# One line of the FFN: the difference of two resident weight granules on GpSimd instead of VectorE

## Chip, cores and metric

The kernel runs on one core of a Trainium2 chip. The metric is the device time of one execution in microseconds; the time of a kernel is the median of its runs. Engines are named as in the profile: PE (TensorE, matmuls) with PEld (its weight loads), DVE (VectorE), ACT (ScalarE), POOL (GpSimd) and SP (SyncE, which issues nearly all DMAs here).

## The reference

One layer of a diffusion backbone in float32: 384 tokens (128 context, 256 latent) of width 2048. adaLN modulation, a mixing sub-layer (gated linear attention beside a Fourier branch) and a SwiGLU FFN with 5632 hidden units. What matters here is the end:

```python
h = rmsnorm(x, lw['norm_pre_ffn']) * (1.0 + sc2) + sh2
ff = (jax.nn.silu(h @ lw['w_ffn_gate']) * (h @ lw['w_ffn_up'])) @ lw['w_ffn_down']
x = x + ga2 * rmsnorm(ff, lw['norm_post_ffn'])
```

## The kernel before

**Split products.** A float32 operand is used as two fp32r parts: ACT casts it to `hi` (`whi`, L1467 in the FFN), DVE makes `lo = src - hi` (`wlo`, L1478), and PE adds up hi·hi, hi·lo and lo·hi. Weights come in granules of 128x1024; each granule that PE uses costs one cast on ACT and one subtraction on DVE. `whi` and `wlo` have four buffers each, so up to four split granules lie ready ahead of PE.

**The FFN** (from about 920 us on) goes through the hidden units in 11 chunks of 512. Chunk 0 is plain. Chunks 1 to 10 compute gate and up with a scheme of fewer products: of the weights it uses granules and their sums and differences, so that seven products stand for eight in the two latent token tiles, while the context tile uses the same granules plainly. With `u` and `g` for up and gate, and 0 and 1 for the halves of the model dimension, the steps of chunk c are, with i = 0..3 for each kind:

- A: `u0` (slot x). B: the difference `g0 - u0`, which is put in x in place of `u0`.
- C: `g1` arrives in `raw`; x becomes `g1 - x` and y becomes `g1 - y` (L1474, L1475). E uses x, F uses y.
- G: `u1` arrives; x becomes `u1 - x` (L1477). H uses x.
- D: the down projection of the chunk before, interleaved with C to H.

PE needs 12 matmuls of 512 columns for an A, B, C or G, 6 for E, F or H, 18 for a D.

**Slots.** The granules of A and B are *resident*: eight slots of 128x1024 in SBUF (tiles named `u`), loaded by SP (L1445) as soon as `free` has them. x and y of a chunk are `slots[slot(0, c, i)]` and `slots[slot(1, c, i)]`; F frees y, H frees x. The other granules come through two `raw` buffers (L1437).

**What sets the order.** All five engines run an order written out by hand. `grab2` (per step) takes a ready granule for PE, runs what is due (`now`), lets SP load (`load_more`) and calls `split_next`, which issues the cast, up to three pending operations (`settle_pend`: evictions of finished PSUM banks, L1588 to L1629), then for this kind of step the differences, then the `wlo`. `split_next` runs about four granules ahead of PE. `sum1(c, i)`, the difference of A's and B's granules, is called early: `sum1(c, 0)` at granule A3, `sum1(c, i + 1)` at granule Bi, each ahead of that granule's `wlo`:

```python
ACT.copy(hi, src)
settle_pend()
if (kind, i) == ("A", 3):
    sum1(c, 0)
elif kind == "B" and i < 3:
    sum1(c, i + 1)
```

A side task, `ada_last` (L1507, L1509, L1531 to L1534), makes the last adaLN vector on DVE from `w_ada`, two DVE instructions a portion, and is stepped at A, G and late D steps, until chunk 9.

POOL does little: a few `memset`s, 15 additions (L1250) and two `wlo` (L228) between 890 and 915 us, and sixteen additions of 128x128 (L1762) in the last 20 us. In the tail, L1724 to L1726 are tiny DVE instructions on 128x1, and L1764 writes the output.

Tiles in SBUF: `u`, `raw`, `whi`, `wlo`, `ep` (gate and up sums), `acc`, `w`, `spad`, `psums` (running down sums), `bias`, `ssq`, `A_hi`, `A_lo`, `x1b`. Tiles in PSUM: `pgu`, `pdn`, `ptr`, `py`, `prow`, `z`, `zx`.

Of the kernel before, what the change touches and what calls it, by code (L numbers as in the profile page):

```python
# [96 lines left out]
def tile_step(ctx: ExitStack, tc: tile.TileContext, a, o):  # L97
    nc = tc.nc
    PE, ACT, DVE, POOL, SP = nc.tensor, nc.scalar, nc.vector, nc.gpsimd, nc.sync
# [776 lines left out]
    with ExitStack() as s:  # L876
# [207 lines left out]
        for b, i in mix_order:  # L1084
# [9 lines left out]
            else:  # L1094
# [4 lines left out]
                g, y = gates.pop((b, i))  # L1099
# [14 lines left out]
    with ExitStack() as s:  # L1114
# [309 lines left out]
        def slot(x, c, i):  # L1424

            return 4 * ((c + x) % 2) + i
# [21 lines left out]

        def sum1(c, i):
            x, y = (slots[slot(n, c, i)] for n in range(2))  # L1450
            DVE.tensor_sub(x, y, x)  # L1451

        def settle_pend():
            for _ in range(3):
# [3 lines left out]
        def split_next():  # L1458

            if not entries:  # L1460
                settle_pend()
                return
            kind, c, i, raw = entries.pop(0)
            x, y = (slots[slot(n, c, i)] if kind not in "RD" else None for n in range(2))
            src = raw if kind in "RCGD" else y if kind == "F" else x
            hi, lo = (wp.tile([P, G], F32R, tag=t, name=t, bufs=4) for t in ("whi", "wlo"))
# [6 lines that stand above are left out]
            elif kind == "C":  # L1473
                DVE.tensor_sub(x, raw, x)  # L1474
                DVE.tensor_sub(y, raw, y)  # L1475
            elif kind == "G":
                DVE.tensor_sub(x, raw, x)  # L1477
            DVE.tensor_sub(lo, src, hi.bitcast(F32))  # L1478
            if kind in "RCGD":
                out_now[0] -= 1  # L1480
            elif kind == "F":
                free.add(slot(1, c, i))
            elif kind == "H":
                free.add(slot(0, c, i))
            ready.append((hi, lo))
# [417 lines left out]
```

## Time and profile before

| what | value |
|---|---|
| time before, median of 3 runs | 1954.05 us (1953.54 to 1954.51) |
| profiled execution, span from first to last instruction | 1950.6 us |
| around the span (median less span) | 3.4 us |
| PE busy | 1936.3 us (99%), 10422 matmuls |
| DVE busy | 1633.1 us (84%), 2114 instructions |
| ACT busy | 906.9 us (46%), 1270 instructions |
| POOL busy | 33.6 us (2%), 55 instructions |
| granted TensorE clock, mean | 0.999 |

"Busy" is the time in which an engine runs at least one instruction; matmuls are pipelined, so 99% says that they follow each other without gaps, not that PE is at its peak. The page gives groups of instructions as `line engine op out<-in shape xcount | busy us, mean ns | idle time ahead of them`. A timeline row is `start us, duration us, engine, line, operation, out<-in, shape, xcount`, with an `x2` or more for instructions in a row that are merged. A row of one line's instructions gives `xcount: min/median/max ns, first to last start`. The profile gives one execution; the time of the program lies above its span by what surrounds it.

### The profile page before, as it was taken

Reading aid. Unit: us, or ns where it says so; the run is one execution under the profiler, and the core shown is the slowest. Engines: PE = TensorE matmul, PEld = TensorE weight load, DVE = VectorE, ACT = ScalarE, POOL = GpSimd, SP = SyncE. Lnnn points to the kernel's source line nnn. Section 1 sums busy time; section 2 is a strip of 40 time slices with the busy share of each in tenths; the row PEclk is TensorE's granted clock in tenths of the full one; section 3 lists DMA queues with packets and bytes.
Section 4 is the critical chain, followed back from the end, with each engine's and each line's share of the span. In section 5 each row is a group of like instructions: output and inputs, shape, how many; then the busy total and the mean of one; then the engine's idle time right before and its main releaser. Section 6 shows DMA issues by size and latency. Waiting matters only on the chain.

```text
span 1950.6 us, 27243 instructions
## 1 busy us (share of the span) xinstructions
PE 1936.3 (99%) x10422; PEld 1705.2 (87%) x10422; DVE 1633.1 (84%) x2114; ACT 906.9 (46%) x1270; POOL 33.6 (2%) x55
## 2 busy tenths in 40 slices
PE   9999999999999999999999999999999999999998
PEld 5779999999889999999988888888888888888886
DVE  5668888878777797977789898999898999887876
ACT  4233554544336654446454444444444444444444
POOL 0000000000000000004000000000000000000001
PEclk9999999999999999999999999999999999999999
DMA  9978677767765786655355535463636263626244
GB/s 391 382 255 272 228 257 239 231 218 244 239 198 178 236 265 212 233 188 210 93 157 162 172 125 179 137 199 112 199 120 209 93 216 98 211 75 194 67 157 144
DMA packets 201179, 380.12 MB, mean 195 GB/s; under 512 B 14160, under 2 KB 127508, under 8 KB 196696
## 3 DMA queue, kind: packets, MB, share of 16 engines
q1 hardware_dynamic: 200520, 378.12, 58.4%
q8 instruction: 82, 1.34, 0.3%
q14 instruction: 49, 0.40, 0.1%
q10 hardware_dynamic: 528, 0.26, 0.0%
HBM read 361.55 MB, written 16.78 MB: 194 GB/s over the span
## 4 chain that ended last, share of the span: by engine, by line
PE 96%; DVE 2%; DMA 2%; ACT 1%; issue 0%; SPq 0%; POOL 0%; DVEq 0%; ACTq 0%; POOLq 0%
PE pmm L261 32%; PE pgu L273 30%; PE pdn L273 18%; PE pfo L273 3%; PE pv L415 3%; PE pgm L398 1%; PE pf L1064 1%; PE pmm L1320 1%; DMA slab<-in_w_ada 1%; PE ptr L1612 1%; PE pf L1065 1%; PE po L673 1%; DMA xraw<-in_w_x 0%; PE px L433 0%; DMA raw<-in_w_d 0%; DVE x1b L1764 0%
## 5 line engine op out<-in xcount | busy, mean ns | idle before, releaser
L261 PE MATMUL pmm<-A_hi,whi 128*128 128x384 f32 x1072 | 361.3, 337 | 0.0
L261 PE MATMUL pmm<-A_hi,wlo 128*128 128x384 f32 x1072 | 358.6, 335 | 0.0
L261 PE MATMUL pmm<-A_lo,whi 128*128 128x384 f32 x1072 | 358.5, 334 | 0.0
L1467 ACT CAST whi<-u 128x1024 fp32r<-128x1024 f32 x200 | 210.6, 1053 | 271.0 <-DVE u L1451 86.2
L227 ACT CAST whi<-raw 128x1024 fp32r<-128x1024 f32 x181 | 189.5, 1050 | 208.1 <-DMA raw<-in_w_gate 69.0
L1467 ACT CAST whi<-raw 128x1024 fp32r<-128x1024 f32 x175 | 184.2, 1053 | 212.1 <-DMA raw<-in_w_g 68.0
L228 DVE TENSOR_TENSOR wlo<-raw,whi 128x1024 fp32r<-128x1024 f32 x179 | 218.1, 1221 | 66.2 <-ACT whi L227 65.5
L1478 DVE TENSOR_TENSOR wlo<-u,whi 128x1024 fp32r<-128x1024 f32 x200 | 243.9, 1220 | 28.1 <-ACT whi L1467 16.9
L273 PE MATMUL pgu<-whi,A_hi 128*128 128x512 f32 x640 | 250.0, 391 | 0.0
L273 PE MATMUL pgu<-whi,A_lo 128*128 128x512 f32 x640 | 249.3, 389 | 0.0
L1478 DVE TENSOR_TENSOR wlo<-raw,whi 128x1024 fp32r<-128x1024 f32 x175 | 213.3, 1219 | 33.9 <-ACT whi L1467 24.6
L600 DVE SCALAR_TENSOR_TENSOR adacc<-adaw,spad,adacc 128x1024 f32<-128x1024 f32 x180 | 222.8, 1279 | 0.3
L261 PEld LDWEIGHTS pmm<-A_hi,whi 128*128 128x128 f32 x1072 | 201.2, 188 | 3.0 <-issue 1.4
L261 PEld LDWEIGHTS pmm<-A_lo,whi 128*128 128x128 f32 x1072 | 201.3, 188 | 0.3
L261 PEld LDWEIGHTS pmm<-A_hi,wlo 128*128 128x128 f32 x1072 | 201.2, 188 | 0.0
L273 PE MATMUL pdn<-whi,hid_hi 128*128 128x512 f32 x480 | 186.9, 389 | 0.0
L273 PE MATMUL pdn<-whi,hid_lo 128*128 128x512 f32 x480 | 186.8, 389 | 0.0
L273 PE MATMUL pgu<-wlo,A_hi 128*128 128x512 f32 x640 | 184.2, 389 | 0.0
L273 PEld LDWEIGHTS pgu<-whi,A_hi 128*128 128x128 f32 x640 | 120.1, 188 | 26.0 <-issue 0.8
L273 PEld LDWEIGHTS pgu<-wlo,A_hi 128*128 128x128 f32 x640 | 120.1, 188 | 25.4
L273 PEld LDWEIGHTS pgu<-whi,A_lo 128*128 128x128 f32 x640 | 120.1, 188 | 25.0
L273 PE MATMUL pgu<-whi,S 128*128 128x512 f32 x480 | 131.1, 395 | 0.0
(386 smaller groups left out, 2900.0 us busy)
## 6 DMA issues: line engine op xcount, KB each, us to landing
adaw<-in_w_ada SPq DMA_DIRECT2D x96, 512.0 KB, 4.1
raw<-in_w_d SPq DMA_DIRECT2D x88, 512.0 KB, 4.6
slab<-in_w_ada SPq DMA_DIRECT2D x32, 1024.0 KB, 10.4
raw<-in_w_gate SPq DMA_DIRECT2D x64, 512.0 KB, 4.7
raw<-in_w_g SPq DMA_DIRECT2D x48, 512.0 KB, 4.2
raw<-in_w_u SPq DMA_DIRECT2D x48, 512.0 KB, 3.8
raw<-in_w_in SPq DMA_DIRECT2D x44, 512.0 KB, 4.2
u<-in_w_u SPq DMA_DIRECT2D x40, 512.0 KB, 4.4
```

The source lines that it names most:

```text
L227: ACT.copy(hi, raw)
L228: sub = lambda: eng.tensor_sub(lo, raw, hi.bitcast(F32))
L261: PE.matmul(dst, w[wi][:, k * n + n0 : k * n + n0 + P], x[xi][:, k0 + k, :], start=first and k == 0 and j == 0, stop=last and k == kts - 1 ...
L273: PE.matmul(dst, stat[x_][m], mov(w[w_], m), start=first and w_ == m == x_ == 0, stop=last and w_ == m == 1,)
L398: PE.matmul(pgv[q : q + 32, :], spad[:, k, :], slab[k // (KT // 2)][:, k % (KT // 2), :], start=k < 4, stop=k >= KT - 4,)
L415: PE.matmul(pv[2 * t + g], hT[x_][:, kb, t * P : (t + 1) * P], w_[:, g * 512 : (g + 1) * 512], start=kb == 0 and j == 0, stop=kb == KT - 1 ...
L600: DVE.scalar_tensor_tensor(acc[:, c, :], w, spad[:, k, c : c + 1], acc[:, c, :], op0=ALU.mult, op1=ALU.add,)
L673: PE.matmul(dst, w[wi], x[xi], start=first and j == 0, stop=last and j == 2)
L1064: PE.matmul(pf[:, 0 : 2 * HT], w[0][:, c], x[k], start=k == 0, stop=False)
L1065: PE.matmul(pf[:, 0:HT], w[1][:, c], x[k][:, 0:HT], start=False, stop=m == 1 and k == 3)
L1467: ACT.copy(hi, src)
L1478: DVE.tensor_sub(lo, src, hi.bitcast(F32))
```

## The change

`sum1` issues its subtraction on POOL. Nothing else is edited. In the order of instructions, the 40 subtractions (4 in each of chunks 1 to 10) leave DVE's queue and stand in POOL's queue in the same order, between its last L228 and its first L1762. Each waits there for the loads of its two granules and for DVE's `wlo` of its A granule. The ACT cast (L1467) of a B granule waits for POOL where it waited for DVE. PE's, ACT's and SP's orders are the same as before.

```diff
         def sum1(c, i):
             x, y = (slots[slot(n, c, i)] for n in range(2))
-            DVE.tensor_sub(x, y, x)
+            POOL.tensor_sub(x, y, x)
```

## Prediction

> **What bounds the kernel now.** I read the head of the page, then the chain of work that ended last, then the busy time by stretches.
>
> ```profile
> span 1950.6 us, 27243 instructions
> ```
> ```profile
> PE 96%; DVE 2%; DMA 2%; ACT 1%; issue 0%; SPq 0%; POOL 0%; DVEq 0%; ACTq 0%; POOLq 0%
> ```
> ```profile
> 960.00:1900.00 940.00, 940.00 (x4255) 776.39 (x4254) 841.54 (x913) 429.47 (x465) 0.00 (x0) 1.00 0.47 149
> 1231.00:1264.00 33.00, 33.00 (x153) 27.30 (x152) 32.42 (x39) 12.26 (x15) 0.00 (x0) 1.00 0.29 94
> ```
>
> The rows of the last fence give, after the length of the stretch, busy time of PE, PEld, DVE, ACT and POOL, then granted clock and DMA. From 960 to 1900 us, where all ten FFN chunks of this change run, PE is busy 940.00 of 940.00 us at a clock of 1.00: matmuls stand back to back, and nothing that another engine gives up can make this stretch shorter. DVE has 841.54 us of work in it (90%) and POOL none. But the mean hides a tight place: in the 33 us around the four differences of chunk 4, DVE is busy 32.42 us. There DVE is the local limit, and PE lives on the four split weight tiles made ahead. So the question is not what DVE saves, but whether the new place of the difference can make a tile arrive later than its **slack**: the time from the end of its wlo instruction (L1478) to the first matmul that reads this wlo.
>
> **The change, part by part.**
>
> ```profile
> L1451 DVE TENSOR_TENSOR u<-u,u x40: 1212/1217/1219, 963.6 to 1816.5; 128x1024 f32<-128x1024 f32 x40
> ```
> ```profile
> L228 POOL TENSOR_TENSOR wlo<-raw,whi 128x1024 fp32r<-128x1024 f32 x2 | 4.8, 2397 | 0.0
> ```
>
> *Removed:* 40 differences on DVE, four in each of ten chunks, 1.217 us each; the next instruction starts 1.13 us after such a one (1245.73 to 1246.86 below), so DVE's queue gets 1.13 us shorter at each, 45 us in all. PE was never short of work in this stretch, so this alone is worth 0.
>
> *Added:* 40 instructions on POOL. The nearest row is the same shape and subtraction on POOL, 2.397 us; I take 2.40. 40 of them make 96 us in 940, on an engine with no work there.
>
> *Moved, and the new waits:* POOL's queue holds nothing but these differences between its last L228 and the sixteen L1762 of the tail, and it issues no DMA. A difference starts as soon as granule A of its pair has been split (both its casts and its wlo) and the loads of both granules are in; on DVE it stood three granules later. So it is ready long before the cast of granule B, which now waits for POOL instead of DVE: in chunk 4 below, A0's wlo ends at 1235.25; 2.40 us later would be 1237.65, where DVE finished this difference at 1246.95. Late results are therefore no cost. The loads into the slots keep their order on SP's queue and stay released by later splits (L1467, L1478). ACT's queue behind that cast is unharmed for the same reason.
>
> *The cost that I do expect:* POOL's work holds up DVE. The row for it is in the tail.
>
> ```profile
> L1725 DVE TENSOR_TENSOR bias<-bias,ssq x3: 160/160/358, 1925.9 to 1938.3; 128x1 f32<-128x1 f32 x3
> ```
> ```profile
> 1938.34 0.36 DVE L1725 TENSOR_TENSOR bias<-bias,ssq 128x1 f32<-128x1 f32 x1
> ```
> ```profile
> 1938.22 0.46 POOL L1762 TENSOR_TENSOR x1b<-x1b,ep 128x128 f32<-128x128 f32 x1 [2.29 <-ACT ep L1761]
> ```
>
> One tiny DVE instruction runs three times: 160, 160 and 358 ns. The long one started 0.12 us into a POOL instruction and ended at 1938.70, 0.02 us after POOL's (1938.68). It reads two tensors from SBUF; so does that POOL instruction. It was held 0.20 us, to about 1938.53, which is 0.15 us before POOL's end. Against it stand DVE instructions that read one tensor from SBUF and the other from PSUM (z, prow, pgu and pdn are PSUM tiles):
>
> ```profile
> L1302 DVE TENSOR_TENSOR A_lo<-z,A_hi x13: 550/557/558, 893.7 to 915.5; 128x384 fp32r<-128x384 f32 x13
> ```
> ```profile
> 907.05 2.40 POOL L228 TENSOR_TENSOR wlo<-raw,whi 128x1024 fp32r<-128x1024 f32 x1
> ```
> ```profile
> 908.04 0.56 DVE L1302 TENSOR_TENSOR A_lo<-z,A_hi 128x384 fp32r<-128x384 f32 x1
> ```
>
> The one at 908.04 lies wholly inside a 2.40 us POOL subtraction and takes its usual time. So I take it that a POOL subtraction holds DVE only where DVE's next instruction reads two SBUF tensors, for up to 2.40 - 0.15 = 2.25 us. This rests on a single held instruction; the bounds of a hold are therefore 0 and 2.40 us.
>
> The Trainium skill, "SBUF — State Buffer", section "Who interferes with whom", states the same as a rule against this change: a VectorE instruction with two SBUF inputs contends with a GpSimd instruction that reads SBUF, through a shared port that is held for a whole instruction, and the second one fully blocks. The long L1725 agrees with it; by the rule to the letter the hold would be 2.40 us, without it 0.
>
> Now the place. DVE's queue in chunk 4, from A0's wlo to B0's (L1478 is the wlo of A0, A1, A2, A3, B0 in turn), and the first matmul that reads B0's wlo:
>
> ```profile
> 1234.03 1.22 DVE L1478 TENSOR_TENSOR wlo<-u,whi 128x1024 fp32r<-128x1024 f32 x1
> 1235.17 1.41 DVE L1509 SCALAR_TENSOR_TENSOR acc<-w,spad,acc 128x512 f32<-128x512 f32 x2
> 1236.49 0.68 DVE L1601 TENSOR_TENSOR ep<-ep,pgu 128x512 f32<-128x512 f32 x1
> 1237.21 0.69 DVE L1601 TENSOR_TENSOR ep<-ep,ep 128x512 f32<-128x512 f32 x1
> ...
> 1238.41 1.22 DVE L1478 TENSOR_TENSOR wlo<-u,whi 128x1024 fp32r<-128x1024 f32 x1
> 1239.55 0.68 DVE L1602 TENSOR_TENSOR ep<-ep,ep 128x512 f32<-128x512 f32 x1
> 1240.15 0.68 DVE L1605 TENSOR_TENSOR ep<-ep,pgu 128x512 f32<-128x512 f32 x1
> 1240.86 0.69 DVE L1605 TENSOR_TENSOR ep<-ep,ep 128x512 f32<-128x512 f32 x1
> 1241.47 1.22 DVE L1478 TENSOR_TENSOR wlo<-u,whi 128x1024 fp32r<-128x1024 f32 x1
> 1242.61 1.41 DVE L1509 SCALAR_TENSOR_TENSOR acc<-w,spad,acc 128x512 f32<-128x512 f32 x2
> 1243.93 1.88 DVE L1629 TENSOR_TENSOR psums<-psums,pdn 128x512 f32<-128x512 f32 x3
> 1245.73 1.22 DVE L1451 TENSOR_TENSOR u<-u,u 128x1024 f32<-128x1024 f32 x1
> 1246.86 1.22 DVE L1478 TENSOR_TENSOR wlo<-u,whi 128x1024 fp32r<-128x1024 f32 x1
> 1248.00 1.41 DVE L1509 SCALAR_TENSOR_TENSOR acc<-w,spad,acc 128x512 f32<-128x512 f32 x2
> 1249.32 1.22 DVE L1451 TENSOR_TENSOR u<-u,u 128x1024 f32<-128x1024 f32 x1
> 1250.46 1.22 DVE L1478 TENSOR_TENSOR wlo<-u,whi 128x1024 fp32r<-128x1024 f32 x1
> ```
> ```profile
> 1253.35 0.61 PE L273 MATMUL pgu<-wlo,S 128*128 128x512 f32 x2
> ```
>
> Each difference starts after the L1478 of its A granule, when DVE's next instruction has already begun; I let POOL have its turn after that one. Difference 0 then falls on the second L1509: held 2.25. Difference 1 starts after L1602; the first L1605 (one operand in PSUM) passes, the second is held 2.25 - 0.65 = 1.6. Differences 2 and 3 each fall on a second L1509: 2.25 each. Sum before B0: 2.25 + 1.6 + 2.25 + 2.25 = 8.35 us. By then two differences have left the queue, 2.27 us. B0's wlo is later by 8.35 - 2.27 = 6.1 us. Its slack is 1253.35 - (1250.46 + 1.22) = 1.67 us, so PE waits 6.1 - 1.7 = **4.4 us** in chunk 4. The tiles after B0 come off better: each drops another 1.13 us, and PE's wait has moved them too.
>
> The other chunks, by DVE's end and PE's first use:
>
> ```profile
> 1059.79 1.22 DVE L1478 TENSOR_TENSOR wlo<-u,whi 128x1024 fp32r<-128x1024 f32 x1
> ...
> 1628.22 1.22 DVE L1478 TENSOR_TENSOR wlo<-u,whi 128x1024 fp32r<-128x1024 f32 x1
> ...
> 1436.14 1.22 DVE L1478 TENSOR_TENSOR wlo<-u,whi 128x1024 fp32r<-128x1024 f32 x1
> ```
> ```profile
> 1064.47 0.61 PE L273 MATMUL pgu<-wlo,S 128*128 128x512 f32 x2
> ...
> 1631.11 0.62 PE L273 MATMUL pgu<-wlo,S 128*128 128x512 f32 x2
> ...
> 1439.51 1.07 PE L273 MATMUL pgu<-wlo,A_hi 128*128 128x512 f32 x4
> ```
>
> Chunk 2, B0: slack 3.46, wait 6.1 - 3.5 = 2.6. Chunk 8, B0: slack 1.67, wait 4.4. Chunk 6 has no L1509 between A3 and B0, so its worst tile is A3: held 2.25 + 1.6 + 2.25 less 1.13 = 5.0, slack 2.15, wait 2.8. In chunks 3, 5, 7, 9 and 10 no L1509 stands behind A0 and A2, as in chunk 7:
>
> ```profile
> 1518.83 0.68 DVE L1601 TENSOR_TENSOR ep<-ep,pgu 128x512 f32<-128x512 f32 x1
> ...
> 1524.94 1.88 DVE L1629 TENSOR_TENSOR psums<-psums,pdn 128x512 f32<-128x512 f32 x3
> ...
> 1531.41 1.22 DVE L1478 TENSOR_TENSOR wlo<-u,whi 128x1024 fp32r<-128x1024 f32 x1
> ```
> ```profile
> 1537.17 0.62 PE L273 MATMUL pgu<-wlo,S 128*128 128x512 f32 x2
> ```
>
> Behind A0 and A2 PSUM readers pass (0.65 and about 1.8 us): holds 1.6 + 1.6 + 0.45 + 2.25 = 5.9, less 2.27, makes 3.6 us against a slack of 4.5: no wait. Chunk 1 runs its first three differences while DVE still idles: no wait. **Sum:** 4.4 + 2.6 + 4.4 + 2.8 = 14.2 us. On the profiled execution 1950.6 + 14.2 = 1964.8 us of span; the median of the runs, 1954.05, lies 3.4 us above that span, for what is around it, so the forecast is 1954.05 + 14.2 = **1968.2 us**.
>
> **The rivals.**
>
> *No hold.* The one long L1725 is chance, or a long POOL instruction lets DVE in. Then DVE is only relieved, PE is full as before, and the time is 1954.0. For it: one row carries the lock. Against it: that row ends with POOL's to 0.02 us, and no other cause is near. This is the case that ends on the other side: not slower, decided by whether L1478 keeps its 1.22 us, and a pair of L1509 its 1.41 us, beside POOL's differences.
>
> *A hold, but DVE keeps its turn.*
>
> ```profile
> L1467 ACT CAST whi<-u 128x1024 fp32r<-128x1024 f32 x200 | 210.6, 1053 | 271.0 <-DVE u L1451 86.2
> ```
>
> Consecutive DVE instructions start some 0.08 us before the one ahead ends (1235.17 before 1235.25), so POOL may get in only at a PSUM reader or a pause. Then L1509 is never held; holds before B0 are 1.6 + 1.6 + 0.45 (1.6 + 1.6 in chunk 2), less 2.27, under every slack. But difference 3 waits until DVE stands at B3 for want of the cast: 2.40 plus the 1.05 us cast, some 3.6, less the 0.9 that DVE is ahead by then, 2.7 late; against slacks of an estimated 0.4, 1.3 and 1.7 us at the next tile, C0 (chunks 4, 6, 8; the same subtraction of DVE's end from PE's first use), PE waits about 5 us: 1959.
>
> *Every difference holds its whole 2.40 us*, whatever stands next: 9.6 - 2.27 = 7.3 late at B0 in nine chunks, less B0's slacks of 1.7 (chunk 4) to an estimated 6.6 us (chunk 3), which the same subtraction gives: about 33 us in all, 1987.
>
> *Faster:* PE is busy 940.00 of 940.00 us of this stretch, so a gain over 0.2% (3.9 us) has nowhere to come from. That the change is not carried out is excluded: the order of instructions has 40 L1451 on POOL and none on DVE.
>
> **How the numbers follow.** The forecast of turns 0.48; DVE keeps its turn 0.17 (1959 is 0.26% up, so 0.10 of it counts as slower and 0.07 as the same); no hold 0.20; whole holds 0.12; faster 0.03. A measurement of this kernel tells about 0.2% from no change. Slower 0.48 + 0.10 + 0.12 = 0.70, same 0.27, faster 0.03. The range takes in no hold at its low end and half of the way from the forecast to whole holds at its high end: 1953.5 to 1981.
>
> **What would show it.** Right: L1451 on POOL near 2.4 us; beside it L1478, L1509 and the second L1601 and L1605 up to 2.2 us longer, L1629 not; waits of PE (or PEld) for wlo L1478 in chunks 2, 4, 6 and 8, none before. Wrong: DVE's durations unchanged beside POOL (no hold), or POOL's instructions stretched and late with DVE's kept (DVE's turn), or PE waiting for ACT's cast behind POOL.

## The result, and the profile after

The changed kernel took 1974.3 us (median of 4 runs, 1973.7 to 1978.0) beside 1953.8 us before (1952.7 to 1954.5): a ratio of 1.0109, 95% interval 1.0097 to 1.0121. It is 20.5 us slower. The forecast was 1968.2 us, 14.2 us slower. The profiled execution has a span 21.1 us longer than before (1971.7 against 1950.6). The page of the changed kernel: span, busy time of the engines, the chain of work that ended last, and the group of the differences.

```profile
span 1971.7 us, 27281 instructions
...
PE 1939.1 (98%) x10422; PEld 1704.6 (86%) x10422; DVE 1654.4 (84%) x2074; ACT 908.4 (46%) x1270; POOL 141.5 (7%) x95
...
PE 89%; DVE 7%; DMA 2%; issue 2%; ACT 1%; SPq 0%; POOL 0%; DVEq 0%; ACTq 0%; POOLq 0%
...
L1451 POOL TENSOR_TENSOR u<-u,u 128x1024 f32<-128x1024 f32 x40 | 107.9, 2697 | 816.2 <-DVE wlo L1478 732.4
```

Two things are to be seen. DVE has 40 instructions fewer (2114 before, 2074 now) and yet 21.3 us *more* busy time (1633.1 before). And the chain, which was 96% PE and 2% DVE, now runs 7% of the span through DVE. POOL itself is nowhere in the chain: it is not late, it makes DVE late. A group mean of 2697 ns instead of 2397 is the first hint that POOL's records hold a wait of their own.

Where PE stands still: busy time from 960 to 1890 us in the changed kernel (columns as in the prediction), and PE's waits in the same stretch (total us, times, longest).

```profile
960.00:1890.00 930.00, 912.03 (x4113) 749.93 (x4112) 836.25 (x849) 417.32 (x452) 101.94 (x38) 1.00 0.46 145
```
```profile
PE pgu L273 <- DVE wlo L1478: 11.3, 7, 2.4
PE ptm L1528 <- DVE psums L1629: 5.0, 3, 1.7
PE pr L1518 <- DVE psums L1629: 1.7, 1, 1.7
```

PE was busy all the time before; now 930 - 912.03 = 18.0 us are missing, and the three rows add up to just that: 11.3 + 5.0 + 1.7 = 18.0. The first row was forecast. The other two were not: `pr` (L1518) and `ptm` (L1528) are the small matmuls of `ada_last`, and they wait for an L1629.

PE's order is the same in both kernels, so the start of each matmul after can be set against its start before. What the difference grows by in each chunk is what the chunk lost (the rest of the 21.1 us: 0.3 ahead of the FFN, 0.1 behind it). The sum is 2.7 us more than the 18.0 us of idle time, some 0.25 us for each of the 11 waits: a matmul is recorded with 0.39 us where the next one starts 0.23 us after it, so a start can move by 0.16 us before any idle time shows, and the start behind the first matmul after a wait is about 0.1 us late too.

| chunk | 2 | 3 | 4 | 5 | 6 | 7 | 8 | 9 | 10 | sum |
|---|---|---|---|---|---|---|---|---|---|---|
| forecast, us | 2.6 | 0 | 4.4 | 0 | 2.8 | 0 | 4.4 | 0 | 0 | 14.2 |
| measured, us | 2.36 | 1.70 | 4.12 | 1.89 | 2.68 | 1.89 | 4.17 | 1.89 | 0 | 20.7 |

The even chunks lose 13.3 us, close to the forecast and a little under it. Chunks 3, 5, 7 and 9 lose 7.4 us that the forecast put at nothing.

**An even chunk, as forecast.** DVE's rows in chunk 4 of the changed kernel that answer to those shown of before, then POOL's four differences, then PE's first use of A3's `wlo` and of B0's.

```profile
1239.53 3.56 DVE L1509 SCALAR_TENSOR_TENSOR acc<-w,spad,acc 128x512 f32<-128x512 f32 x2
...
1246.66 0.68 DVE L1605 TENSOR_TENSOR ep<-ep,pgu 128x512 f32<-128x512 f32 x1
1247.38 2.18 DVE L1605 TENSOR_TENSOR ep<-ep,ep 128x512 f32<-128x512 f32 x1
...
1250.62 3.54 DVE L1509 SCALAR_TENSOR_TENSOR acc<-w,spad,acc 128x512 f32<-128x512 f32 x2
1254.08 1.87 DVE L1629 TENSOR_TENSOR psums<-psums,pdn 128x512 f32<-128x512 f32 x3
...
1257.01 3.55 DVE L1509 SCALAR_TENSOR_TENSOR acc<-w,spad,acc 128x512 f32<-128x512 f32 x2
1260.48 1.21 DVE L1478 TENSOR_TENSOR wlo<-u,whi 128x1024 fp32r<-128x1024 f32 x1
```
```profile
1239.69 2.84 POOL L1451 TENSOR_TENSOR u<-u,u 128x1024 f32<-128x1024 f32 x1 [80.46 <-DVE wlo L1478]
1246.22 2.79 POOL L1451 TENSOR_TENSOR u<-u,u 128x1024 f32<-128x1024 f32 x1 [3.69 <-DVE wlo L1478]
1250.78 2.83 POOL L1451 TENSOR_TENSOR u<-u,u 128x1024 f32<-128x1024 f32 x1 [1.76 <-DVE wlo L1478]
1257.17 2.84 POOL L1451 TENSOR_TENSOR u<-u,u 128x1024 f32<-128x1024 f32 x1 [3.56 <-DVE wlo L1478]
```
```profile
1257.14 1.20 PE L273 MATMUL pgu<-wlo,A_hi 128*128 128x512 f32 x4 [1.98 <-DVE wlo L1478]
...
1261.75 0.73 PE L273 MATMUL pgu<-wlo,S 128*128 128x512 f32 x2 [1.59 <-DVE wlo L1478]
```

Read them together: the pair of L1509 took 1.41 us before and takes 3.54 to 3.56 now, three times, each time with a difference beside it. The first L1605, which reads PSUM, passes in 0.68 us; the second, with both operands in SBUF, takes 2.18 instead of 0.69. The holds are 2.15 + 1.49 + 2.13 + 2.14 = 7.9 us; less the 2.27 us of the two differences that left the queue, B0's `wlo` is 5.6 us late, and with its slack of 1.67 us PE loses 4.0. It loses them in two waits, 1.98 us for A3 and, since that has moved PE already, 1.59 us more for B0; the table, by the starts, has 4.1.

**An odd chunk, not as forecast.** Chunk 5: DVE and PE before, then DVE and PE after.

```profile
1330.66 0.69 DVE L1601 TENSOR_TENSOR ep<-ep,ep 128x512 f32<-128x512 f32 x1
...
1334.32 0.69 DVE L1605 TENSOR_TENSOR ep<-ep,ep 128x512 f32<-128x512 f32 x1
...
1336.06 1.87 DVE L1629 TENSOR_TENSOR psums<-psums,pdn 128x512 f32<-128x512 f32 x3
```
```profile
1338.17 0.27 PE L1528 MATMUL ptm<-ident,adev 128*128 128x128 f32 x1
```
```profile
1339.15 2.40 DVE L1601 TENSOR_TENSOR ep<-ep,ep 128x512 f32<-128x512 f32 x1
...
1344.53 2.17 DVE L1605 TENSOR_TENSOR ep<-ep,ep 128x512 f32<-128x512 f32 x1
...
1347.76 1.87 DVE L1629 TENSOR_TENSOR psums<-psums,pdn 128x512 f32<-128x512 f32 x3
```
```profile
1348.49 0.33 PE L1528 MATMUL ptm<-ident,adev 128*128 128x128 f32 x1 [1.67 <-DVE psums L1629]
```

`ptm` is written to a PSUM bank that held a `pdn`, and L1629 is the reader that gives the bank free. Before, the first of the three L1629 ended at about 1336.7 (1336.06 and the usual 0.68 us), 1.4 us ahead of `ptm`. In the changed kernel differences 0 and 1 hold the second L1601 (0.69 to 2.40) and the second L1605 (0.69 to 2.17), 3.2 us together. Nothing has left the queue by then, since on DVE difference 0 stood behind L1629. 3.2 less 1.4 is 1.8 us, and PE waits 1.7.

### The profile page after: what moved, and what is told of

The parts are those of the page before. It is cut to its first block, busy times and chain, and to the rows that moved or that the text cites. A ratio compares the mean times of both kernels' runs of the same rounds, so it can differ in the third digit from the quotient of the medians.

```text
span 1971.7 us, 27281 instructions
## 1 busy us (share of the span) xinstructions
PE 1939.1 (98%) x10422; PEld 1704.6 (86%) x10422; DVE 1654.4 (84%) x2074; ACT 908.4 (46%) x1270; POOL 141.5 (7%) x95
## 4 chain that ended last, share of the span: by engine, by line
PE 89%; DVE 7%; DMA 2%; issue 2%; ACT 1%; SPq 0%; POOL 0%; DVEq 0%; ACTq 0%; POOLq 0%
PE pmm L261 32%; PE pgu L273 25%; PE pdn L273 16%; PE pfo L273 3%; PE pv L415 3%; DVE wlo L1478 2%; DVE acc L1509 2%; PE pgm L398 1%; PE pf L1064 1%; PE pmm L1320 1%; DMA slab<-in_w_ada 1%; PE ptr L1612 1%; PE pf L1065 1%; DVE ep L1601 1%; DMA xraw<-in_w_x 1%
## 5 line engine op out<-in xcount | busy, mean ns | idle before, releaser
L1467 ACT CAST whi<-u 128x1024 fp32r<-128x1024 f32 x200 | 210.6, 1053 | 262.3 <-PE pgu L273 103.5
L1467 ACT CAST whi<-raw 128x1024 fp32r<-128x1024 f32 x175 | 184.2, 1053 | 214.6 <-DMA raw<-in_w_g 69.0
L1478 DVE TENSOR_TENSOR wlo<-u,whi 128x1024 fp32r<-128x1024 f32 x200 | 250.3, 1257 | 26.4 <-ACT whi L1467 13.7
L228 DVE TENSOR_TENSOR wlo<-raw,whi 128x1024 fp32r<-128x1024 f32 x179 | 218.3, 1222 | 63.6 <-ACT whi L227 63.0
L1478 DVE TENSOR_TENSOR wlo<-raw,whi 128x1024 fp32r<-128x1024 f32 x175 | 213.7, 1221 | 34.4 <-ACT whi L1467 24.1
L1451 POOL TENSOR_TENSOR u<-u,u 128x1024 f32<-128x1024 f32 x40 | 107.9, 2697 | 816.2 <-DVE wlo L1478 732.4
```

Of the source, the lines that this page charges most:

```text
L228: sub = lambda: eng.tensor_sub(lo, raw, hi.bitcast(F32))
L1451: POOL.tensor_sub(x, y, x)
```

## The experiments

Two theories stood at the start. *Hold:* a POOL instruction that reads SBUF keeps DVE's next instruction from running, if that one reads two SBUF tensors, and the time lost is what such a hold pushes past the slack of a tile or a bank. *Hand-over:* the loss comes from results changing engines (ACT's cast waits for POOL) or from any long POOL instruction. Line numbers below can differ by some lines where an edit adds some.

**Holds without a hand-over.** The differences stay on DVE; POOL multiplies x by ones, in place, as soon as A's `wlo` is made.

```diff
             DVE.tensor_sub(lo, src, hi.bitcast(F32))
+            if kind == "A":
+                x8 = x.rearrange("p (a b) -> p a b", b=P)
+                POOL.tensor_mul(x8, x8, ones.unsqueeze(1).to_broadcast([P, 8, P]))
```

> The differences stay on DVE; POOL gets a useless instruction of the same size in their place: behind each A granule's wlo it multiplies that granule in its slot by ones (two SBUF inputs, 128x1024, 40 times). Nothing of POOL's is late for anyone: DVE's difference stands three granules later. Theory of the hold: POOL's instruction takes 2.4 to 3.3 us and DVE's next instruction with two SBUF inputs is held to its end, just as in the changed kernel, while DVE is not relieved of 1.13 us each; so it is worse than the changed kernel's +20.5 us: chunk 4 by 8.35 less 0.4 at C0, about 8, chunks 8 and 6 about 7, chunk 2 about 5, the odd ones 1.8 to 2.7, some +34 us (1988). Rival, that the hand-over from POOL to the cast costs the time: no hand-over here, 1954.

Measured: 1992.3 us, ratio 1.0202 (1.0185 to 1.0219). The busy times from 960 to 1890 us:

```profile
960.00:1890.00 930.00, 904.99 (x4034) 739.01 (x4033) 864.46 (x871) 404.52 (x442) 100.58 (x38) 0.99 0.46 143
```

PE lacks 25.0 us here, with no difference moved: POOL's work beside DVE is enough, and DVE waits for no result of POOL. PE lacks more than in the changed kernel, because DVE isn't relieved of the differences. The 39.0 us by which this kernel is slower (34 were expected) are not all waits. The granted clock, which stays at 1.00 in this stretch of the changed kernel, is at 0.50 here in four pieces of 17 us together; 39 matmuls start in them, 0.43 us apart instead of 0.23, which makes an estimated 8 us; most of what is left is the 0.25 us around each wait. The last section comes back to the clock.

**POOL busy, but only writing.** One 128x1 copy and six `memset`s of 128x352 at the same place.

```diff
+        scr = pf.tile([P, 352], F32, name="scr")
...
+            if kind == "A":
+                POOL.tensor_copy(scr[:, 0:1], lo[:, 0:1].bitcast(F32))
+                for _ in range(6):
+                    POOL.memset(scr, 0.0)
```

> As read2, but POOL reads one column of the wlo (128x1) and then only writes: six memsets of 128x352 into a scratch tile, 2.3 us in all by the 0.42 us of a 128x384 memset. Theory of the hold (only a POOL instruction that reads SBUF holds DVE): DVE's durations beside the memsets stay at 1.22 and 0.74 us, under 0.2 us more behind each tiny copy, time 1954 to 1955. Rival, that any work of POOL beside DVE slows it: as much as read2, +20 us or more.

Measured: 1956.9 us, 1.0018 (1.0009 to 1.0028). DVE's rows for `wlo` (L1479 here) and the side task's additions (L1514 here):

```profile
L1479 DVE TENSOR_TENSOR wlo<-u,whi x200: 1208/1219/1229, 949.8 to 1891.0; 128x1024 fp32r<-128x1024 f32 x100
```
```profile
L1514 DVE SCALAR_TENSOR_TENSOR acc<-w,spad,acc x120: 739/745/750, 972.0 to 1691.2; 128x512 f32<-128x512 f32 x120
```

No DVE instruction is held (maximum 1229 and 750 ns; 3411 and 2894 in the changed kernel). The 3.6 us were not expected, so the same was run without the `memset`s:

> As the kernel with the memsets on POOL, but without them: the scratch tile and one copy of 128x1 per A granule stay. If the 3.6 us of that kernel came from the memsets, this takes 1953 to 1954; if from the tile's place or the tiny copies, it takes 1957 again.

Measured: 1957.2 us, 1.002 (1.0011 to 1.003). The two agree to 0.01 us in the start of each chunk, so the `memset`s cost nothing. What is left, 0.37 us in each chunk with PE busy 930.00 of 930.00 us, comes from the scratch tile or the tiny copies; which of them stays open.

**A POOL instruction with one input.** POOL copies x onto itself.

```diff
+            if kind == "A":
+                POOL.tensor_copy(x, x)
```

> As read2, but POOL copies the granule in place: one SBUF input, 128x1024. Its time on POOL is not known here: between the 0.96 us of a memset of this size and 2.4 us. If every POOL instruction that reads SBUF holds a DVE instruction with two SBUF inputs, the DVE instruction behind it ends with it and the loss lies between 0 and read2's; with 1.2 us of POOL it is 3 to 8 us. Rival, that only a POOL instruction with two inputs holds: DVE's durations unchanged, 1954.

Measured: 1959.1 us, 1.0031 (1.0021 to 1.0041). The side task's additions in this kernel:

```profile
L1511 DVE SCALAR_TENSOR_TENSOR acc<-w,spad,acc x120: 733/744/1528, 972.3 to 1693.7; 128x512 f32<-128x512 f32 x120
```

A copy reads one tensor, and still a hold appears: 1528 instead of 744 ns. It is shorter, as the copy is (1351 ns mean on POOL against 2674 for the product above).

**Half a difference.** DVE makes columns 0 to 511, POOL the rest.

```diff
-            DVE.tensor_sub(x, y, x)
+            DVE.tensor_sub(x[:, 0:512], y[:, 0:512], x[:, 0:512])
+            POOL.tensor_sub(x[:, 512:G], y[:, 512:G], x[:, 512:G])
```

> Each difference is cut: DVE makes the first 512 columns, POOL the other 512 (1.3 us by the rows of 384 and 1024 columns). Theory: a hold lasts as long as POOL's instruction, so about 1.2 us instead of 2.3; before B0 in chunks 4 and 8 it is 1.2 + 0.55 + 1.2 + 1.2 less 2 x 0.53, 3.1 against 1.7 of slack, 1.4 each; chunk 6 0.3; chunk 2 and the odd ones nothing, as the L1629 are late by 1.1 where 3.2 cost 1.8. Some +3 us, 1957. Rival, a fixed cost for each POOL instruction whatever its length: +20 us again.

Measured: 1956.7 us, 1.0015 (1.0006 to 1.0024). PE's waits in the stretch:

```profile
PE pgu L273 <- DVE wlo L1479: 1.3, 2, 0.6
```

Half the work on POOL costs far less than half of 20 us: what stays under a tile's slack is free. Over the ten chunks the matmuls lose 2.4 us, 1.2 in chunk 4, 0.4 in chunk 6 and 0.9 in chunk 8.

**The odd chunks alone, in two parts.** The condition in the first kernel is `c in (3, 5, 7, 9) and i < 2`, in the second `c in (3, 5, 7, 9) and i > 1`.

```diff
-            DVE.tensor_sub(x, y, x)
+            (POOL if c in (3, 5, 7, 9) and i < 2 else DVE).tensor_sub(x, y, x)
```

> Only differences 0 and 1 of chunks 3, 5, 7 and 9 are made by POOL, 8 of the 40. Theory (the reading of the changed kernel's trace): they hold L1478 by some 1.8 us each, so L1629 frees its PSUM bank late and the small matmuls of ada_last (L1518, L1528) wait 1.8 us once in each of these chunks, 4 x 1.8 = +7.2 us, about 1961, with no wait of PE for wlo. Rival (these chunks cost nothing, as the prediction had it): 1954, and the loss of the changed kernel lies wholly in the even chunks.

Measured: 1961.5 us, 1.004 (1.0025 to 1.0055), +7.6 us. PE's waits in the stretch, all of them, and the `wlo` row:

```profile
PE ptm L1528 <- DVE psums L1629: 5.0, 3, 1.7
PE pr L1518 <- DVE psums L1629: 1.7, 1, 1.7
```
```profile
L1478 DVE TENSOR_TENSOR wlo<-u,whi x200: 1210/1220/1228, 951.5 to 1896.3; 128x1024 fp32r<-128x1024 f32 x100
```

The two unforeseen rows of the changed kernel, to the tenth, and nothing else. The losses by chunk are 1.75, 1.88, 1.89 and 1.88 us. One word of the expectation was wrong: no `wlo` is held (maximum 1228 ns); what these two differences hold is L1601 and L1605, as in the rows of chunk 5.

> Only differences 2 and 3 of chunks 3, 5, 7 and 9 are made by POOL, 8 of the 40. Theory: they hold DVE as long as the others, but L1629 stands ahead of them and what they hold has slack, so the time stays at 1954 and L1518 and L1528 wait for nothing new. Rival (a fixed price for each difference on POOL, the changed kernel's +20.5 us over 40): 8 x 0.51 = +4 us, 1958.

Measured: 1953.5 us, 0.9999 (0.999 to 1.0008). As the theory says: eight differences on POOL, no time lost. A price for each difference is out.

**The even chunks alone.**

```diff
+            (POOL if c in (2, 4, 6, 8) else DVE).tensor_sub(x, y, x)
```

> Only the differences of chunks 2, 4, 6 and 8 are made by POOL, 16 of the 40. Theory: the waits of PE for wlo come back alone, some +12.4 to 13.2 us, 1966 to 1967, and together with the kernel of differences 0 and 1 of the odd chunks they make up the changed kernel's +20.5. Rival (a fixed price for each difference): 16 x 0.51 = +8 us, 1962.

Measured: 1969.5 us, 1.0078 (1.0063 to 1.0093), +15.6 us. PE's waits and busy time in the stretch:

```profile
PE pgu L273 <- DVE wlo L1478: 11.3, 7, 2.4
```
```profile
960.00:1890.00 930.00, 918.70 (x4141) 756.55 (x4140) 833.93 (x874) 419.59 (x453) 45.54 (x16) 1.00 0.47 146
```

The waits are the forecast ones: 11.3 us, the same row as in the changed kernel. PE's missing time adds up: 11.3 us here and 6.7 in the first kernel of the odd chunks make the 18.0 of the changed one. The losses by chunk are 2.34, 4.17, 4.29 and 4.13 us, 14.9 in all: as in the changed kernel but for chunk 6, with 1.6 us more, which the last section takes up. Of the rest of this profiled execution's excess over the one before (17.4 us in all), 2.2 us lie ahead of the FFN.

**What stands behind the difference.** If the place decides, moving the side task must move the loss. The first attempt kept all differences on POOL and dropped the side task's steps at A.

```diff
-        rate[0] = 0.85
+        rate[0] = 1.28
...
-                if kind in "AG":
+                if kind == "G":
                     step(ada)
```

> All differences on POOL as in the changed kernel, but DVE's steps of ada_last stand behind the G steps alone, at a rate of 1.28 in place of 0.85, and no longer behind the A steps. Theory: with no L1509 behind a difference the holds in the even chunks fall on fewer and shorter instructions, and most of the 12.4 us of waits for wlo go; the odd chunks may keep their 7.2: 1956 to 1963. Rival (a price per difference, whatever stands behind it): 1974 again.

Measured: 1994.6 us, 1.0211 (1.0194 to 1.0228). The expectation failed because the edit did not do what it was meant for. DVE in chunk 5 of this kernel:

```profile
1343.39 3.56 DVE L1509 SCALAR_TENSOR_TENSOR acc<-w,spad,acc 128x512 f32<-128x512 f32 x2
...
1351.24 2.17 DVE L1605 TENSOR_TENSOR ep<-ep,ep 128x512 f32<-128x512 f32 x1
...
1354.47 3.54 DVE L1509 SCALAR_TENSOR_TENSOR acc<-w,spad,acc 128x512 f32<-128x512 f32 x2
```

POOL starts a difference when A's `wlo` is made, and the L1509 behind A0 and A2 come from the steps at G and late D, not from those at A. With these steps denser, the costly order of an even chunk now stands in chunks 5, 7 and 9 as well (and no longer in 8). The same order with the differences on DVE shows what the order itself costs:

> The counterpart of the kernel that took 1994.6: ada_last stepped behind the G steps and the last four D steps (rate 1.28), the differences on DVE as before. Theory: the 40 us of that kernel are holds (its trace has the costly order, L1509 behind the wlo of A0 and A2, in the odd chunks too), so this one takes 1953 to 1956. Rival: the other order alone makes DVE late, 1970 to 1990 without any instruction on POOL.

Measured: 1961.2 us, 1.0039 (1.0024 to 1.0054). The order alone costs 8 us, which neither theory had, and POOL's differences 33 us on top of it. By the two traces, PE's waits from 960 to 1890 us grow by 20.8 us (from 6.5 to 27.3), and with POOL at work the clock is at 0.50 in six pieces of 3.4 us, 48 matmuls 0.2 us late each, an estimated 10 us more. So the failed attempt is evidence after all: costly order in more chunks, more loss.

The second attempt steps the side task at B and C only. No L1509 then stands behind A0 and A2 in any chunk; in chunks 3 to 10 POOL's difference meets the second L1601 there, or a PSUM reader.

```diff
-        rate[0] = 0.85
+        rate[0] = 1.28
...
-                if not last_c and i >= 4:
-                    step(ada)
...
-                if kind in "AG":
+                if kind in "BC":
                     step(ada)
```

> All 40 differences on POOL, and ada_last stepped behind the B and C steps alone (rate 1.28), so that no L1509 stands behind the wlo of an A granule and its small matmuls stand far from L1629. Theory (what a hold costs is decided by the DVE work that stands behind it): every chunk then looks like an odd chunk without pr and ptm, no wait of PE for wlo and none for L1629 is left, and the time is that of the same edit with the differences on DVE, within 2 us: about 1954. Rival (a price per difference, wherever it stands): 20 us above that kernel, 1974.

> The counterpart: ada_last stepped behind the B and C steps alone, the differences on DVE as before. Both theories: DVE's work is the same in another order and PE has no wait there, 1953 to 1956.

Measured: 1966.2 us with the differences on POOL, 1.0069 (1.0054 to 1.0084), and 1966.1 us with them on DVE, 1.0069 (1.0052 to 1.0085). The absolute times were missed: this order costs 13 us by itself (in the kernel with the differences on DVE, PE waits 7.8 us from 960 to 1890 us, 3.8 of them at the small matmuls). But the question was the difference between the two, and it is 0.1 us, where either median is known to about 3 us. The two profiled executions are finer: PE waits 9.0 us with POOL at work and 7.8 us without, 1.2 us more. In the kernel with POOL, the second L1601 and L1509:

```profile
L1601 DVE TENSOR_TENSOR ep<-ep,ep x10: 693/2399/2403, 1048.6 to 1906.7; 128x512 f32<-128x512 f32 x10
```
```profile
L1509 DVE SCALAR_TENSOR_TENSOR acc<-w,spad,acc x120: 736/742/753, 978.5 to 1576.5; 128x512 f32<-128x512 f32 x120
```

The holds are all there on L1601 (median 2399 ns where 690 is usual), none falls on L1509, and they cost PE about 1 us where the changed kernel lost 20.7. The engine rows of the two pages, with POOL and then with DVE:

```profile
PE 1939.6 (99%) x10422; PEld 1704.8 (87%) x10422; DVE 1646.4 (84%) x2074; ACT 907.4 (46%) x1270; POOL 143.1 (7%) x95
```
```profile
PE 1938.8 (99%) x10422; PEld 1704.5 (87%) x10422; DVE 1633.6 (83%) x2114; ACT 907.3 (46%) x1270; POOL 33.6 (2%) x55
```

DVE carries 12.8 us more with POOL at work, at almost the same time of the kernel. This rules out a tempting reading of the first page, that the kernel got 20.5 us slower because DVE has 21.3 us more to do. No version that was run beats the kernel before by more than can be measured.

## Why the prediction was right and where it was not

- *PE is the bound, and the question is whether a tile comes too late.* Right: PE's missing 18.0 us are its waits for DVE.
- *The removed work is worth nothing.* Right as far as tested: no kernel with fewer differences on DVE is measurably faster.
- *Late results are no cost.* Right: PE waits for no result of POOL, nor for ACT behind POOL.
- *A POOL subtraction holds DVE's next instruction with two SBUF tensors.* Right. Beside the 40 differences, 39 DVE instructions are over 0.25 us longer than usual. The forecast hold was 2.25 us, the measured one 2.13 to 2.15 on a pair of L1509. L1629, with one operand in PSUM, kept its time. The rule cited from the Trainium skill, "SBUF — State Buffer", section "Who interferes with whom", agrees with these rows; its 2.40 us to the letter (the whole instruction) is 0.25 us more than a pair of L1509 lost.
- *POOL has its turn after the instruction in progress.* Right in the changed kernel: the first L1509 of a pair runs, the second is held, and no difference lasts more than 3317 ns, 0.94 us over the shortest, less than one L1478. The rival in which DVE keeps its turn asked for L1509 never held, and falls; so do no hold, and whole holds (1987 us).
- *The even chunks lose 4.4, 2.6, 4.4 and 2.8 us.* Right in mechanism, a little high: 13.3 measured against 14.2, because each hold was 0.1 us shorter.
- ***The odd chunks lose nothing.* This step failed.** It set 3.6 us of delay against the 4.5 us slack of B0's `wlo`, and so it compared one consumer only. The holds themselves came as forecast (5.9 us in a chunk; chunk 5 has 1.71 + 1.48 on L1601 and L1605, 0.62 on L1478 and 2.22 on L1533, 6.0 in all), and no `wlo` came late there. DVE's queue feeds PE in two ways: by the tiles it makes and by the banks it frees. The small matmuls of `ada_last` in chunks 3, 5, 7 and 9 follow the first L1629 with 1.4 us of slack (1.5 in chunk 3), and the holds of differences 0 and 1 are 3.2 us. That makes 1.8 us in each of four chunks, and 7.4 measured, which the kernel with only these eight differences on POOL shows alone (+7.6). 14.2 - 0.9 + 7.4 = 20.7 us, the sum of the table.
- *The range, 1953.5 to 1981.* The measured 1974.3 us lies in it, and that is luck in part: the upper margin was meant for whole holds, which fall, and it was used up by waits for banks, which the prediction does not have. And half of the way from 1968.2 to 1987 is 1977.6, not the 1981 that is given; the measured time lies under both.

## What to carry to other kernels

Before work is moved to GpSimd beside a busy VectorE, write down for each moved instruction which VectorE instruction will stand behind it, and whether that one reads two tensors from SBUF: the moved time then comes back on VectorE, here at about twice what was taken away for a pair of L1509 (2.15 us against 1.13). Such a delay costs nothing while it stays under the slack, so check every consumer of the delayed queue: tiles that it makes, and banks or buffers that it frees. A mean share of busy time, or an engine's total, says nothing about it: 12.8 us more DVE work cost PE about 1 us in one order, and 3.2 us at the wrong place cost 1.8 us in each of four chunks.

## What the runs showed of the hardware that was not expected

**A hold doesn't need two inputs on either side.** A POOL copy with one input held DVE (above), a `memset` did not. In the changed kernel a DVE instruction with one SBUF tensor and a column of scalars was held too, once (2630 ns), and so was a tiny one of 128x8 each time (170 ns before):

```profile
L1507 DVE TENSOR_SCALAR acc<-w,spad x8: 476/479/2630, 966.2 to 1547.8; 128x512 f32<-128x512 f32 x8
```
```profile
L1533 DVE TENSOR_TENSOR mods<-mods,cols_b x4: 2176/2390/2392, 1157.1 to 1739.9; 128x8 f32<-128x8 f32 x4
```

**POOL's record holds its own wait for a turn.** In the changed kernel the differences take 2382 ns at the least and 3317 at the most, the more the longer DVE's instruction in progress still runs, if that one reads two SBUF tensors: about 2.79 us with 0.52 us of an L1602 to go, 3.31 us with 1.06 us of an L1478. With 0.52 us of an L1601 to go that reads PSUM, it stays at 2.41 us. All forty in one row:

```profile
L1451 POOL TENSOR_TENSOR u<-u,u x40: 2382/2784/3317, 951.7 to 1835.9; 128x1024 f32<-128x1024 f32 x40
```

Once, in the kernel stepped at G and D (1994.6 us), DVE did keep its turn: POOL's record spans three of the four L1478 merged in the DVE row, each with its usual 1.21 us, and ended 2.3 us after the last. Why this one was passed over is open.

```profile
1462.80 5.58 POOL L1451 TENSOR_TENSOR u<-u,u 128x1024 f32<-128x1024 f32 x1 [4.88 <-DVE wlo L1478]
```
```profile
1461.51 4.62 DVE L1478 TENSOR_TENSOR wlo<-u,whi 128x1024 fp32r<-128x1024 f32 x4
```

**A longer pause of PE can cost more than itself.** In chunk 6 PE pauses 2.4 us in the changed kernel and in the kernel of the even chunks alike. Busy times of the 3.2 us that follow, in the one and in the other (granted clock is the third column from the end):

```profile
1452.40:1455.60 3.20, 3.16 (x14) 2.63 (x15) 3.20 (x2) 1.07 (x2) 3.13 (x1) 1.00 0.00 0
```
```profile
1452.00:1455.20 3.20, 3.20 (x9) 2.54 (x8) 3.20 (x2) 1.77 (x3) 2.09 (x1) 0.52 0.00 0
```

The same pause, and once the clock stays at 1.00, once it falls to 0.52; these are the 1.6 us by which chunk 6 differs (eight matmuls start 0.2 us late each). The Trainium skill, "TensorE: Matmul & The Clock Gate", section "Part 1: The HAM clock gate (the "warmup" mystery)", has the clock halved after an idle window of about 3.4 us that runs free of the kernel.

The traces agree with the length and with the free running, but the window need not be idle throughout. In all fourteen traces the granted clock changes only at whole multiples of 3.41 us, counted from its first change. The pause, 2.39 us long, falls into one such window in the kernel of the even chunks (1448.27 to 1451.68 us, PE busy 1.02 of 3.41 us). In the changed kernel the edge of a window at 1450.66 us cuts it in two (PE busy 2.80 us ahead of the edge, 1.63 us behind it). From 960 to 1890 us, over all traces, a window with 1.94 us or more of idle time was followed by a window at half the clock each time, 11 times in three kernels; one with 1.84 us or less never took the clock down. So whether a pause of this length costs more than itself was decided here by where it fell.
